# Second layer's channel mixer of a hybrid trunk: two up units on the scaled input, rstd applied to their rows, and the last gate's adaLN steps as rows on VectorE

## Chip, core and metric

One core of one Trainium2 chip runs the whole program. The metric is the device time of one execution in microseconds (us), as the median of three runs. Engines are named as in the profile: PE is TensorE's matmul, PEld its weight load, DVE is VectorE, ACT is ScalarE, POOL is GpSimd, SP is SyncE, whose queue issues the weight loads.

## What is computed

Two layers over 256 tokens of width 1024. Each layer has a token mixer (three branches, left out here) and a channel mixer. Both start from an RMS norm that is modulated (adaLN) by six vectors of 1024 numbers, computed from a condition vector `c`:

```python
c_act = jax.nn.silu(c)
for l in range(DEPTH):
    mod = c_act @ w_mod[l] + b_mod[l]
    sh1, sc1, g1, sh2, sc2, g2 = jnp.split(mod, 6, axis=-1)
    ...
    x = x + g1[:, None, :] * y
    h = modulate(rms_norm(x, ffn_norm_g[l]), sh2, sc2)
    x = x + g2[:, None, :] * channel_mixer(h, w_up[l], ffn_dw_w[l], ffn_dw_b[l], w_down[l])

def channel_mixer(h, w_up, ffn_dw_w, ffn_dw_b, w_down):
    u = causal_depthwise_conv(h @ w_up, ffn_dw_w, ffn_dw_b)   # width 3
    a, b = jnp.split(u, 2, axis=-1)                           # 2816 each
    return (jax.nn.silu(a) * b) @ w_down
```

The norm's factor rstd is one number for each token. So `h @ w_up` is also `rstd * ((gain * x) @ w_up) + sh2 @ w_up`: the product can start before rstd is known, if rstd is applied to its result and the shift's product is added. That identity is what the changed code uses for two units.

## The kernel before

**Layout.** Channels lie on the 128 partitions and tokens along the free dimension. `x` is 8 tiles (k = 0 to 7) of 128 x 256. The channel mixer's inner width of 2816 is cut into 22 units (j = 0 to 21). `up(j)` makes 128 channels of a and 128 of b; `down(j)` adds unit j's product with `w_down` to 8 output tiles in four PSUM tiles.

**Weights.** A weight load (`wload`, SP's queue) brings 512 KB to a `raw` tile. `split` makes its high half on ACT (`whi`, L222) and the rest on DVE (`wlo`, L224). A product takes three matmuls: high x high and low x high as it goes (L300, L301), and all high x low last (L303). One weight load feeds 24 matmuls, called a unit load here: an `up` takes two unit loads (k = 0 to 3, then 4 to 7), a `down` one. `take` hands out loads in a fixed list (`all_units`) and splits two ahead of their use; the `raw`, `whi` and `wlo` tiles rotate through few buffers, so a load or a split waits until a buffer is let go. L294 to L296 are the three matmuls of the last products of an accumulation, done bank after bank.

**Between the token mixer and the channel mixer.** `project` ends in four PSUM tiles. DVE adds them, gated, to `x` (L1251), ACT squares (L530), DVE adds squares in pairs (L540), PE sums over partitions (L545), DVE and POOL make rstd (L519, L520), PE spreads it over the partitions (L555, `bcast_rows`), and then each of 8 `norm_tile` steps takes DVE, ACT, DVE (L603, L604, L605) and gives `hh` and `hl`, the halves of h. While this chain runs, PE has nothing to multiply but `mod_part(l, 5)` (L407: the vector g2, 8 steps, each with its own 512 KB load of `in_wm`) and filler matmuls on a constant (`warm`, L322).

**After an `up`.** ACT scales and biases the PSUM tile (L1298), DVE adds the two shifted taps (L1300, twice for each of a and b), ACT makes the tanh (L1304), DVE multiplies (L1305, L1306), ACT and DVE write the high and low half that `down(j)` reads (L1308, L1309; tile `mhl`). Three PSUM buffers (`psb`) serve the `up` units, so `up(j+3)` waits until the taps of `up(j)` have been read. Five buffers (`psa`) serve the accumulations.

**Order.** The list `FFN` sets how `up` and `down` alternate: up 0, 1, 2, down 0, up 3, 4, down 1, up 5, down 2 and so on, so `up` runs three ahead and later four. A scheduler with a cost model of its own turns the program into one fixed row of instructions for each engine; `tc.issue_after` adds edges to it. On the chip every engine goes through its row in order.

**adaLN as rows.** Where (layer, vector) stands in `ROWS`, the vector is made on DVE: `mod_row` loads 512 KB of transposed weights and does one multiply with a running sum over 1024 elements (L390) and one add (L391), 8 times for a vector. In layer 0's channel mixer 16 such steps for the next layer run beside `up` and `down`.

Of the kernel before, what the change touches and what calls it, by code (L numbers as in the profile page):

```python
# [64 lines left out]
ROWS = [(0, 0), (0, 1), (1, 0), (1, 1), (1, 2)] + RPARTS  # L65
# [68 lines left out]
FFN = []  # L134
for _j in range(NF):
    for _u in range(NF):
        if (1, _u) not in FFN and _u <= _j + (3 if _j >= FLEAD else 2):
# [16 lines left out]
def trunk_kernel(ctx, tc, xT, crow, ccol, pos, invf, modb_d, cols_d, grow_d, wmh, wmr, wm, win1, wqkv,  # L154
# [60 lines left out]
    def split(raw, lead):  # L215
# [7 lines left out]
        with tc.issue_after(hold[0]) if hold[0] else ExitStack():  # L223
            ve.tensor_tensor(lo, raw, hi.bitcast(F32), op=ALU.subtract)  # L224
# [63 lines left out]
    def flush(whole=False):  # L288
        if whole:
# [233 lines left out]
    def sq_sums(srcs, bank=None):  # L523
# [3 lines left out]
        alone = SHORT and n == 8  # L527
        for k, src in enumerate(srcs):
            sq = e1()
            ac.activation(sq, src, AF.Square)  # L530
# [12 lines left out]
            with tc.issue_after(warm(bank, WARM1[0]).ins) if bank is not None and WARM1[0] and k == n - 2 + (not alone) else ExitStack():  # L543
# [8 lines left out]
    def bcast_rows(r):  # L552
        bc = psb()
        for b in range(NB):
            rows_last[0] = te.matmul(bc[:, b * P:(b + 1) * P], r[:, b:b + 1].to_broadcast([P, P]), ident,  # L555
                                     start=True, stop=True)
# [44 lines left out]
    def norm_tile(k, bc, gs, sh, hh, hl):  # L601
        t = e1()
        ve.scalar_tensor_tensor(t, x[:, k, :], gs, bc, op0=ALU.mult, op1=ALU.mult)  # L603
# [1 line left out]
        v = ve.scalar_tensor_tensor(hl[:, k, :], t, sh, hh[:, k, :].bitcast(F32), op0=ALU.add, op1=ALU.subtract)  # L605
# [135 lines left out]
    def layer(l):  # L741
# [508 lines left out]
        for n in range(KD):  # L1250
# [3 lines left out]

        gs2 = mod_gain(l, 4, "ffn_g")
        fill = mod_part(l, 5)
        bc = norm_stats(fill)
        hh, hl = new_h()
        marks = [norm_tile(k, bc, gs2[:, k:k + 1], mod[l][:, 24 + k:25 + k], hh, hl) for k in range(KD)]
        fw = wk.tile([P, 3, 44], F32, tag="fw", name=nm("fw"), bufs=1)  # L1260
        fb = wk.tile([P, 44], F32, tag="fb", name=nm("fb"), bufs=1)
        with tc.issue_after(marks[0][1].ins):
# [21 lines left out]
        lo_tags[:] = [("wlo", 4), ("qkT", 2), ("wlo", 4), ("kv", 2)] if l else [("wlo", 4), ("qkT", 2), ("wlo", 4), ("kv", 2), ("wlo", 4), ("qkT", 2), ("wlo", 4), ("thc", 1)]  # L1284
        def up(j):
            pp = psb()
            for _ in range(2):
                for k, w in take()[0]:
                    for i in range(2):
                        mmw(pp[:, i * S:(i + 1) * S], cut(w, i, P), (hh[:, k, :], hl[:, k, :]), k == 0 and i == 0,  # L1290
                            k == KD - 1 and i == 1)
                flush()
# [132 lines left out]
```

## Time and profile before

| | |
|---|---|
| time, median of 3 runs | 907.75 us (905.73 to 909.3) |
| the profiled execution: time, span | 909.82 us, 907.7 us |
| PE busy, DVE busy, ACT busy over the span | 98%, 88%, 61% |
| projection of layer 1 ends on PE | 711.5 us |
| first matmul of layer 1's `up(0)` | 718.93 us |
| layer 1's `down(1)` starts, `up(5)` starts | 751.93 us, 754.76 us |
| last matmuls of the program | about 904 us |

Times are from the span's start. A row of the timeline reads: start, duration, engine, line, operation, output tile <- input tiles, shape, count, and in brackets the idle time before it with what ended it. The durations of neighbouring rows overlap a little, because each instruction's record reaches into the next one's start; what an instruction costs its engine is read from start to start. A busy PE in the table of stretches is not a PE at its peak either, since its records overlap by more than half.

### The profile page before, as it was taken

The page shows a single profiled execution, that of the slowest core. Times are in us where ns is not written, and L with a number is a line of the kernel's source. Part 1 is how long each engine was busy: PE and PEld are TensorE (multiplying, and loading weights), DVE is VectorE, ACT ScalarE, POOL GpSimd, SP SyncE. Part 2 cuts the span into 40 slices and gives each one's busy share as a digit, 9 for nine tenths or more (in the row PEclk, how much of TensorE's full clock was granted, in tenths as well). Part 3 has the DMA queues.
Part 4 walks back from the last instruction along what each step waited for, and adds up shares of the span by engine and source line. Part 5 has one row for each costly group of instructions (what it writes and reads, how often), then busy time and mean ns, then how long its engine had stood idle before and what let it go on. Part 6 is the DMA issues. An engine that isn't in the chain of part 4 may idle for free.

```text
span 907.7 us, 18736 instructions
## 1 busy us (share of the span) xinstructions
PE 888.3 (98%) x7339; PEld 841.5 (93%) x7339; DVE 797.1 (88%) x1554; ACT 555.2 (61%) x979; POOL 46.2 (5%) x36
## 2 busy tenths in 40 slices
PE   7999999999999999999999999999999999999998
PEld 6888888999998999999989988989999899999998
DVE  6989999999988999998764999999887798777774
ACT  4677588644755655556543676986475565565551
POOL 1010700000000000000000043000000000000000
PEclk9999999999999999999999999999999999999999
DMA  8956535699988889996633664157768676566631
GB/s 321 379 196 202 187 118 183 214 334 320 304 292 308 295 296 312 313 301 211 200 112 108 197 223 161 53 184 244 264 206 270 221 259 189 186 194 199 190 92 47
DMA packets 57976, 201.59 MB, mean 222 GB/s; under 512 B 6944, under 2 KB 8480, under 8 KB 57888
## 3 DMA queue, kind: packets, MB, share of 16 engines
q1 hardware_dynamic: 57888, 200.41, 66.6%
q8 instruction: 57, 0.93, 0.4%
q14 instruction: 31, 0.25, 0.1%
HBM read 199.33 MB, written 1.05 MB: 221 GB/s over the span
## 4 chain that ended last, share of the span: by engine, by line
PE 78%; DVE 12%; ACT 4%; DMA 3%; issue 2%; SPq 0%; POOL 0%; POOLq 0%; DVEq 0%; ACTq 0%
PE psb L300 16%; PE psb L301 16%; PE psb L303 15%; PE psa L300 7%; PE psa L301 7%; PE psa L303 7%; DVE wlo L224 3%; DVE cacc L1103 3%; PE psa L407 2%; DVE raw L778 1%; ACT whi L222 1%; PE psa L294 1%; DVE raw L390 1%; DMA raw<-in_win 1%; ACT p L675 1%
## 5 line engine op out<-in xcount | busy, mean ns | idle before, releaser
L222 ACT ACTIVATE whi<-raw 128x1024 fp32r<-128x1024 f32 (+2 forms) x286 | 296.6, 1043 | 217.6 <-PE psb L301 117.3
L224 DVE TENSOR_TENSOR wlo<-raw,whi 128x1024 fp32r<-128x1024 f32 (+2 forms) x286 | 340.3, 1195 | 65.5 <-ACT whi L222 57.9
L300 PE MATMUL psb<-hh,whi 128*128 128x256 f32 x1088 | 263.5, 282 | 0.5 <-ACT p L675 0.3
L301 PE MATMUL psb<-hl,whi 128*128 128x256 f32 x1088 | 261.0, 280 | 0.0
L300 PEld LDWEIGHTS psb<-hh,whi 128*128 128x128 f32 x1088 | 205.0, 189 | 6.3 <-issue 3.8
L301 PEld LDWEIGHTS psb<-hl,whi 128*128 128x128 f32 x1088 | 205.0, 189 | 0.5 <-DVE wlo L224 0.4
L303 PE MATMUL psb<-hh,wlo 128*128 128x256 f32 x1088 | 149.2, 279 | 0.0
L303 PEld LDWEIGHTS psb<-hh,wlo 128*128 128x128 f32 x1088 | 135.6, 188 | 0.8 <-issue 0.8
L1103 DVE SCALAR_TENSOR_TENSOR cacc<-upad,cw,cacc 128x256 f32<-128x256 f32 x240 | 105.7, 477 | 0.4
L300 PE MATMUL psa<-mhl,whi 128*128 128x256 f32 x400 | 94.0, 278 | 0.0
L301 PE MATMUL psa<-mhl,whi 128*128 128x256 f32 x400 | 93.7, 278 | 0.0
L1300 DVE SCALAR_TENSOR_TENSOR e<-psb,fw,e 128x255 f32<-128x255 f32 (+1 forms) x176 | 84.0, 477 | 5.4 <-ACT e L1298 4.5
L520 POOL TENSOR_TENSOR rs<-rs,mhalf 128x8 f32<-128x8 f32 (+3 forms) x26 | 44.6, 1729 | 669.2 <-DVE rs L519 669.1
L300 PEld LDWEIGHTS psa<-mhl,whi 128*128 128x128 f32 x400 | 75.0, 188 | 0.0
L301 PEld LDWEIGHTS psa<-mhl,whi 128*128 128x128 f32 x400 | 75.0, 188 | 0.0
L1298 ACT ACTIVATE e<-psb,fb,fw 128x256 f32<-128x256 f32 x88 | 48.5, 551 | 22.4 <-DVE e L1300 19.2
L390 DVE SCALAR_TENSOR_TENSOR raw<-raw,crow 128x1024 f32<-128x1024 f32 x48 | 58.5, 1218 | 0.5 <-DMA raw<-in_wmr 0.5
L303 PE MATMUL psa<-mhl,wlo 128*128 128x256 f32 x400 | 53.9, 277 | 0.0
L303 PEld LDWEIGHTS psa<-mhl,wlo 128*128 128x128 f32 x400 | 49.4, 188 | 0.0
L1308 ACT ACTIVATE mhl<-e 128x256 fp32r<-128x256 f32 x44 | 18.3, 416 | 30.1 <-DVE e L1306 27.6
L300 PE MATMUL psb<-whi,hh 128*128 128x416 f32 (+1 forms) x96 | 30.9, 350 | 4.5 <-ACT hh L854 4.5
L301 PE MATMUL psb<-whi,hl 128*128 128x416 f32 (+1 forms) x96 | 29.6, 343 | 0.2 <-DVE hl L855 0.2
(275 smaller groups left out, 1474.3 us busy)
## 6 DMA issues: line engine op xcount, KB each, us to landing
raw<-in_wup SPq DMA_DIRECT2D x88, 512.0 KB, 4.9
raw<-in_wmr SPq DMA_DIRECT2D x60, 512.0 KB, 5.7
raw<-in_wdn SPq DMA_DIRECT2D x44, 512.0 KB, 4.5
raw<-in_wm SPq DMA_DIRECT2D x32, 512.0 KB, 4.7
raw<-in_wgab SPq DMA_DIRECT2D x32, 512.0 KB, 4.9
raw<-in_wqkv SPq DMA_DIRECT2D x24, 512.0 KB, 5.1
raw<-in_win SPq DMA_DIRECT2D x16, 512.0 KB, 4.7
raw<-in_wgc SPq DMA_DIRECT2D x16, 512.0 KB, 4.3
```

The source lines that it names most:

```text
L222: ac.activation(hi, raw, AF.Copy)
L224: ve.tensor_tensor(lo, raw, hi.bitcast(F32), op=ALU.subtract)
L300: te.matmul(o, p1[0], p1[1], start=start, stop=False)
L301: te.matmul(o, p2[0], p2[1], start=False, stop=False)
L303: te.matmul(o, p3[0], p3[1], start=False, stop=stop)
L390: ve.scalar_tensor_tensor(raw, raw, scale, row, op0=ALU.mult, op1=ALU.mult, accum_out=acc)
L407: te.matmul(acc[32 * c:32 * c + 32, 0:S], cact[:, k:k + 1].to_broadcast([P, 32]), raw[:, c * S:(c + 1) * S], start=(k == 0), stop=(k == KD ...
L520: gp.tensor_tensor(r, r, mhalf[:, :n], op=ALU.pow)
L1103: ve.scalar_tensor_tensor(aj, upad[:, j, t:t + S], cw[:, j * 31 + t:j * 31 + t + 1], aj, op0=ALU.mult, op1=ALU.add)
L1298: ac.activation(t, src, AF.Identity, scale=fw[:, 2, c:c + 1], bias=fb[:, c:c + 1])
L1300: ve.scalar_tensor_tensor(t[:, d:S], src[:, 0:S - d], fw[:, 2 - d, c:c + 1], t[:, d:S], op0=ALU.mult, op1=ALU.add)
L1308: ac.activation(mh, th, AF.Copy)
```

## The change

In layer 1 alone, the channel mixer's start is rewritten. `raw_tile` forms u = gain * x (without rstd) in high and low halves as soon as a tile of `x` is complete, 256 columns and two more that hold the shift (`raw_operand`). `up(0)` and `up(1)` (`NRAW = 2`) multiply that u, 258 columns wide, each into two `psa` tiles, half by half: `raw_unit(0)`, `raw_unit(1)`, the sums over partitions, `raw_unit(0)` again, the spreading of rstd, `raw_unit(1)` again. Their results are multiplied by rstd's row on DVE, and the shift's product (column 256) is added on ACT. `norm_tile` still makes `hh` and `hl`, now for `up(2)` onward. The filler matmuls and `mod_part(1, 5)` leave PE; g2 comes from eight `mod_row` steps. `bcast_rows` uses a transpose in place of a matmul with the identity. The order of layer 1 becomes up 0 to 4, down 0, up 5, down 1, up 6: `up` runs four ahead from the start.

```diff
-ROWS = [(0, 0), (0, 1), (1, 0), (1, 1), (1, 2)] + RPARTS
+ROWS = [(0, 0), (0, 1), (1, 0), (1, 1), (1, 2), (1, 5)] + RPARTS
...
-            FFN.append((1, _u))
-    FFN.append((0, _j))
+NRAW = 2
+FFN = [_ffn(2, 3), _ffn(4, 4)]
...
     def split(raw, lead):
-        with tc.issue_after(hold[0]) if hold[0] else ExitStack():
+        after = holds.pop(0) if holds else hold[0]
+        with tc.issue_after(after) if after else ExitStack():
             ve.tensor_tensor(lo, raw, hi.bitcast(F32), op=ALU.subtract)
...
+            if l == 1:
+                for i in range(2):
+                    for j in range(NRAW):
+                        yield *chop(wup[l, j], KD, S)[i], LEAD
...
     def bcast_rows(r):
-            rows_last[0] = te.matmul(bc[:, b * P:(b + 1) * P], r[:, b:b + 1].to_broadcast([P, P]), ident,
-                                     start=True, stop=True)
+            rows_last[0] = te.transpose(bc[:, b * P:(b + 1) * P], r[:, b:b + 1].to_broadcast([P, P]), ident)
...
+    def raw_tile(k, gs, uh, ul):
+        ac.activation(uh[k][:, 0:S], x[:, k, :], AF.Identity, scale=gs[:, k:k + 1])
+        return ve.scalar_tensor_tensor(ul[k][:, 0:S], x[:, k, :], gs[:, k:k + 1], uh[k][:, 0:S].bitcast(F32),
+                                       op0=ALU.mult, op1=ALU.subtract)
...
+        else:
+            taps()
+            uh, ul = raw_operand(mod[l][:, 24:32])
+            st = psb()
+            sums = []
+            for n in range(KD):
+                residual(n)
+                sq = e1()
+                ac.activation(sq, x[:, n, :], AF.Square)
+                if n % 2:
+                    ve.tensor_tensor(sums[-1], sums[-1], sq, op=ALU.add)
+                else:
+                    sums.append(sq)
+                last = raw_tile(n, gs2, uh, ul)
+            pre.extend([psa(), psa()] for _ in range(NRAW))
+
+            def raw_unit(j):
+                for k, w in take()[0]:
+                    for i in range(2):
+                        mmw(pre[j][i][:, 0:S + 2], cut(w, i, P), (uh[k], ul[k]), k == 0, k == KD - 1)
+                return flush()
...
+            holds[:] = [last.ins]
+            mid = raw_unit(0)
+            holds.clear()
+            behind[0] = 1
+            with tc.issue_after(mid.ins):
+                mid = raw_unit(1)
+            for i in range(4):
+                with tc.issue_after(mid.ins):
+                    mid = total(i)
+            r = rstd_of(st[:, 0:NB], NB, 1.0 / D)
+            holds[:] = [rst[0].ins]
+            with tc.issue_after(mid.ins):
+                mid = raw_unit(0)
+            holds.clear()
+            with tc.issue_after(mid.ins):
+                bc = bcast_rows(r)
+            hh, hl = new_h()
+            for k in range(KD):
+                marks.append(norm_tile(k, bc, gs2[:, k:k + 1], mod[l][:, 24 + k:25 + k], hh, hl,
+                                       marks[k - 2] if k > 1 else None))
+            holds[:] = [marks[3][1].ins]
+            with tc.issue_after(rows_last[0].ins):
+                raw_unit(1)
...
-        rows_left = [(1, r, k) for r in range(2) for k in range(KD)] if l == 0 else []
+        rows_left = [(1, r, k) for r in ((5,) if l else range(2)) for k in range(KD)]
...
+                if raw:
+                    src = e1()
+                    ve.tensor_tensor(src, pre[j][i][:, 0:S], bcs, op=ALU.mult)
+                    cb = small(1, "m0", 4)
+                    ve.tensor_copy(cb, pre[j][i][:, S:S + 1])
+                    ac.activation(src, src, AF.Identity, bias=cb)
+                else:
+                    src = pp[:, i * S:(i + 1) * S]
...
-            if j > 1 and rows_left:
+            if j > (8 if l else 1) and rows_left:
                 mod_row(crow1[0], *rows_left.pop(0), scale=0.5 if CDMA else 1.0)
```

The fixed rows of the engines show where this puts the work. In the changed kernel the matmul lines 300, 301, 303 are 317, 318, 320 and `split`'s DVE line 224 is 231; the evacuation's lines 1300, 1305, 1306, 1309 are 1409, 1414, 1415, 1418. The number behind a name only tells tiles apart.

TensorE right behind layer 1's projection, before (`psa_1574_9317` is the sum of `mod_part(1, 5)`, `psb_1578_9331` that of the squares):

```order
L296 MATMUL psa_1502_8812<-mhl_1558_9179,wlo_1562_9188 128x256
L407 MATMUL psa_1574_9317<-raw_1575_9318,cact_106 32x256 x4
L407 MATMUL psa_1574_9317<-raw_1576_9324,cact_106 32x256 x4
L545 MATMUL psb_1578_9331<-ones_84,e1_1579_9332 128x1 x2
L545 MATMUL psb_1578_9331<-ones_84,e1_1581_9339 128x1 x2
```

The same place in the changed kernel (`psa_1590_9371` and `psa_1591_9372` are the a and b halves of `up(0)`, `u_1576_9315` and `u_1578_9317` hold u's high and low half):

```order
L313 MATMUL psa_1502_8812<-mhl_1558_9179,wlo_1562_9188 128x256
L317 MATMUL psa_1590_9371<-u_1576_9315,whi_1564_9193 128x258
L318 MATMUL psa_1590_9371<-u_1578_9317,whi_1564_9193 128x258
L317 MATMUL psa_1591_9372<-u_1576_9315,whi_1564_9193 128x258
L318 MATMUL psa_1591_9372<-u_1578_9317,whi_1564_9193 128x258
```

The products of `up(0)` stand directly behind the projection; the sums of squares come 48 matmuls later.

VectorE around the low half of the second unit's activation, before (`mhl_1628_9605`, read by `down(1)`):

```order
L417 TENSOR_TENSOR mod1_101<-psa_1630_9610,modb_94 128x8
L1306 TENSOR_TENSOR e1_1627_9601<-e1_1627_9601,e1_1626_9597 128x256
L1300 SCALAR_TENSOR_TENSOR e1_1638_9675<-psb_1631_9614,fw_1605_9450,e1_1638_9675 128x255
L1309 TENSOR_TENSOR mhl_1628_9605<-e1_1627_9601,mhl_1628_9605 128x256
L1300 SCALAR_TENSOR_TENSOR e1_1638_9675<-psb_1631_9614,fw_1605_9450,e1_1638_9675 128x254
```

The same place in the changed kernel (`mhl_1632_9588` is read by `down(1)`; `psb_1633_9591` is the PSUM tile of `up(2)`, `wlo_1688_9936` belongs to `down(2)` and `wlo_1692_9967` to `up(7)`):

```order
L231 TENSOR_TENSOR wlo_1688_9936<-raw_1686_9933,whi_1687_9935 128x1024
L1409 SCALAR_TENSOR_TENSOR e1_1630_9580<-e1_1628_9575,fw_1573_9307,e1_1630_9580 128x255
L1414 SCALAR_TENSOR_TENSOR e1_1631_9584<-e1_1631_9584,e1_1627_9571 128x256
L1409 SCALAR_TENSOR_TENSOR e1_1630_9580<-e1_1628_9575,fw_1573_9307,e1_1630_9580 128x254
L1409 SCALAR_TENSOR_TENSOR e1_1642_9656<-psb_1633_9591,fw_1573_9307,e1_1642_9656 128x255
L1415 TENSOR_TENSOR e1_1631_9584<-e1_1631_9584,e1_1630_9580 128x256
L1409 SCALAR_TENSOR_TENSOR e1_1642_9656<-psb_1633_9591,fw_1573_9307,e1_1642_9656 128x254
L231 TENSOR_TENSOR wlo_1692_9967<-raw_1690_9964,whi_1691_9966 128x1024
L1418 TENSOR_TENSOR mhl_1632_9588<-e1_1631_9584,mhl_1632_9588 128x256
L1409 SCALAR_TENSOR_TENSOR e1_1643_9660<-psb_1633_9591,fw_1573_9307,e1_1643_9660 128x255
L1414 SCALAR_TENSOR_TENSOR e1_1644_9664<-e1_1644_9664,e1_1642_9656 128x256
L1409 SCALAR_TENSOR_TENSOR e1_1643_9660<-psb_1633_9591,fw_1573_9307,e1_1643_9660 128x254
```

The second unit's half now stands among the taps of `up(2)` and behind a split for `up(7)`; the last of the rows lets go the PSUM buffer that `up(5)` takes.

TensorE at `down(1)`, before (`psb_1660_9800` is `up(4)`):

```order
L303 MATMUL psb_1660_9800<-hh_1595_9416,wlo_1652_9728 128x256 x8
L300 MATMUL psa_1642_9690<-mhl_1628_9605,whi_1654_9757 128x256
L301 MATMUL psa_1642_9690<-mhl_1628_9605,whi_1654_9757 128x256
L300 MATMUL psa_1642_9690<-mhl_1628_9605,whi_1654_9757 128x256
L301 MATMUL psa_1642_9690<-mhl_1628_9605,whi_1654_9757 128x256
L300 MATMUL psa_1643_9691<-mhl_1628_9605,whi_1654_9757 128x256
L301 MATMUL psa_1643_9691<-mhl_1628_9605,whi_1654_9757 128x256
```

The same place in the changed kernel (`mhl_1624_9563` is the activation of `down(0)`, `psb_1675_9857` is `up(5)`):

```order
L317 MATMUL psa_1668_9823<-mhl_1632_9588,whi_1673_9829 128x256
L317 MATMUL psa_1669_9824<-mhl_1632_9588,whi_1673_9829 128x256
L317 MATMUL psa_1670_9825<-mhl_1632_9588,whi_1673_9829 128x256
L317 MATMUL psa_1671_9826<-mhl_1632_9588,whi_1673_9829 128x256
L318 MATMUL psa_1668_9823<-mhl_1632_9588,whi_1673_9829 128x256
L317 MATMUL psa_1668_9823<-mhl_1632_9588,whi_1673_9829 128x256
L318 MATMUL psa_1668_9823<-mhl_1632_9588,whi_1673_9829 128x256
L318 MATMUL psa_1669_9824<-mhl_1632_9588,whi_1673_9829 128x256
L317 MATMUL psa_1669_9824<-mhl_1632_9588,whi_1673_9829 128x256
L318 MATMUL psa_1669_9824<-mhl_1632_9588,whi_1673_9829 128x256
L317 MATMUL psb_1675_9857<-hh_1603_9475,whi_1659_9750 128x256
```

Ten matmuls of `down(1)`, of which the fifth is the first to read the low half, now stand directly behind `down(0)` and ahead of `up(5)`.

More of the change, by code (lines that the diff above doesn't have):

```diff
@@ L130, with _ffn @@
 NCOL = _o
[L134 to L137, printed above, removed]
-            FFN.append((1, _u))
-    FFN.append((0, _j))
+def _ffn(first, then):
+    o = []
+    for j in range(NF):
+        for u in range(NF):
+            if (1, u) not in o and u <= j + (then if j >= FLEAD else first):
+                o.append((1, u))
+        o.append((0, j))
+    return o
+NRAW = 2
+FFN = [_ffn(2, 3), _ffn(4, 4)]
 def _two_pi_parts():
@@ L207, in trunk_kernel @@
     hold = [None]
+    holds = []
     raw_tags = [("raw", 4)]
@@ L302, in flush @@
         for o, _, _, p3, _, stop in queue:
-            te.matmul(o, p3[0], p3[1], start=False, stop=stop)
+            last = te.matmul(o, p3[0], p3[1], start=False, stop=stop)
         queue.clear()
+        return last
     def cut(w, i, n):
@@ L542, in sq_sums @@
                     continue
-            with tc.issue_after(warm(bank, WARM1[0]).ins) if bank is not None and WARM1[0] and k == n - 2 + (not alone) else ExitStack():
+            with tc.issue_after(warm(bank, WARM1[0]).ins) if bank is not None and WARM1[0] and k == n - 1 else ExitStack():
                 for b in range(NB):
@@ L1249, in layer, with residual, taps @@
         ve.tensor_scalar(g1h, mod[l][:, 16:24], 0.5, None, op0=ALU.mult)
-        for n in range(KD):
+        def residual(n):
             ve.scalar_tensor_tensor(x[:, n, :], acc[n // 2][:, (n % 2) * S:(n % 2 + 1) * S], g1h[:, n:n + 1],
                                     x[:, n, :], op0=ALU.mult, op1=ALU.add)
[L1255 to L1262, printed above, removed]
+        def taps():
             wsrc = cv(l, "fdw_w").rearrange("p (t j) -> p t j", t=3)
@@ L1283, in layer @@
         hi_tags[:] = [("whi", 4), ("mq", 3)]
-        lo_tags[:] = [("wlo", 4), ("qkT", 2), ("wlo", 4), ("kv", 2)] if l else [("wlo", 4), ("qkT", 2), ("wlo", 4), ("kv", 2), ("wlo", 4), ("qkT", 2), ("wlo", 4), ("thc", 1)]
+        lo_tags[:] = [("wlo", 4), ("qkT", 2), ("wlo", 4), ("kv", 2), ("wlo", 4), ("qkT", 2), ("wlo", 4), ("thc", 1)]
         def up(j):
[L1286 to L1292, printed above, removed]
+            raw = j < len(pre)
+            if not raw:
+                pp = psb()
+                for _ in range(2):
+                    for k, w in take()[0]:
+                        for i in range(2):
+                            mmw(pp[:, i * S:(i + 1) * S], cut(w, i, P), (hh[:, k, :], hl[:, k, :]), k == 0 and i == 0,
+                                k == KD - 1 and i == 1)
+                    flush()
             ab = []
```

82 lines of the change are left out of this document (63 added, 19 removed).

## The prediction

> **What bounds the kernel now.** I read the page first, for which engine the end hangs on, then the stretches, to see whether that holds around the change, then the timelines of TensorE and VectorE from layer 1's projection to `down(1)`.
>
> ```profile
> PE 888.3 (98%) x7339; PEld 841.5 (93%) x7339; DVE 797.1 (88%) x1554; ACT 555.2 (61%) x979; POOL 46.2 (5%) x36
> PE 78%; DVE 12%; ACT 4%; DMA 3%; issue 2%; SPq 0%; POOL 0%; POOLq 0%; DVEq 0%; ACTq 0%
> 360.00:380.00 20.00, 20.00 (x179) 20.00 (x178) 20.00 (x40) 10.73 (x17) 0.00 (x0) 1.00 0.94 310
> 720.00:740.00 20.00, 19.88 (x175) 18.55 (x174) 19.41 (x35) 14.34 (x23) 0.00 (x0) 1.00 0.76 253
> 780.00:800.00 20.00, 20.00 (x176) 20.00 (x175) 15.52 (x26) 11.99 (x18) 0.00 (x0) 1.00 0.60 189
> ```
>
> Line 1 and the chain (line 2, 78% PE) say TensorE. But a mean hides the stage: in the rows of stretches (PE, PEld, DVE, ACT, POOL, then PEclk, DMA share and GB/s) VectorE is busy 19.41 of 20 us at 720 to 740, right behind the place of the change, and 15.52 at 780 to 800. So TensorE bounds, with VectorE nearly full for some 25 us. What counts is which of the two the change loads there.
>
> ```profile
> 711.24 0.28 PE L296 MATMUL psa<-mhl,wlo 128*128 128x256 f32 x1
> 711.45 1.07 PE L407 MATMUL psa<-raw,cact 128*32 128x256 f32 x16
> 712.45 1.05 PE L545 MATMUL psb<-ones,e 128*128 128x1 f32 x8
> 713.36 0.60 PE L322 MATMUL psb<-warm_w 128*128 128x256 bf16 x4
> 713.95 1.05 PE L545 MATMUL psb<-ones,e 128*128 128x1 f32 x8
> 714.87 0.93 PE L322 MATMUL psb<-warm_w 128*128 128x256 bf16 x7
> 716.10 0.71 PE L555 MATMUL psb<-ident,rs 128*128 128x128 f32 x4 [0.30 <-POOL rs L520]
> 716.64 0.49 PE L322 MATMUL psb<-warm_w 128*128 128x256 bf16 x3
> 718.93 0.39 PE L300 MATMUL psb<-hh,whi 128*128 128x256 f32 x1
> 751.93 0.28 PE L300 MATMUL psa<-mhl,whi 128*128 128x256 f32 x1
> 754.76 0.28 PE L300 MATMUL psb<-hh,whi 128*128 128x256 f32 x1
> 788.67 0.28 PE L300 MATMUL psb<-hh,whi 128*128 128x256 f32 x1
> 791.39 0.28 PE L300 MATMUL psb<-hh,whi 128*128 128x256 f32 x1
> ```
>
> TensorE's timeline: the projection's last matmul ends at 711.52, `up(0)` starts at 718.93, `down(1)` at 751.93, `up(5)` at 754.76. One unit load lies between the last two: 2.83 us for 24 matmuls, or 0.118 each; between 788.67 and 791.39 it is 2.72. So much for TensorE: 40.41 us from 711.52 to 751.93 hold 11 unit loads (up 0 to 4, `down(0)`), 31.1 us, and 9.3 us of other things.
>
> ```profile
> 707.50 0.87 DVE L1251 SCALAR_TENSOR_TENSOR x<-psa,g1h,x 128x256 f32<-128x256 f32 x2
> 715.04 0.16 DVE L519 TENSOR_SCALAR rs<-psb 128x2 f32<-128x2 f32 x1 [0.81 <-PE psb L545]
> 716.85 1.26 DVE L603 SCALAR_TENSOR_TENSOR e<-x,gs,psb 128x256 f32<-128x256 f32 x3 [1.64 <-PE psb L555]
> 718.03 0.88 DVE L605 SCALAR_TENSOR_TENSOR hl<-e,mod,hh 128x256 fp32r<-128x256 f32 x2
> 724.72 3.48 DVE L224 TENSOR_TENSOR wlo<-raw,whi 128x1024 fp32r<-128x1024 f32 x3
> 728.13 0.47 DVE L1300 SCALAR_TENSOR_TENSOR e<-psb,fw,e 128x255 f32<-128x255 f32 x1
> 728.52 1.21 DVE L224 TENSOR_TENSOR wlo<-raw,whi 128x1024 fp32r<-128x1024 f32 x1
> 731.57 0.41 DVE L1305 SCALAR_TENSOR_TENSOR e<-e,e 128x256 f32<-128x256 f32 x1
> 731.91 0.47 DVE L1300 SCALAR_TENSOR_TENSOR e<-psb,fw,e 128x254 f32<-128x254 f32 x1
> 734.89 1.23 DVE L224 TENSOR_TENSOR wlo<-raw,whi 128x1024 fp32r<-128x1024 f32 x1 [0.59 <-ACT whi L222]
> 741.17 0.42 DVE L1309 TENSOR_TENSOR mhl<-e,mhl 128x256 fp32r<-128x256 f32 x1
> ```
>
> VectorE's timeline, start to start: a split 3.41 / 3 = 1.137, a norm step 1.18 / 3 = 0.393 (716.85 to 718.03), a tap 0.39, a multiply 0.34. From the norm's first step to the half that `down(1)` reads (L1309 at 741.17) it takes 24.3 us with 0.59 idle. TensorE comes to `down(1)` 10.4 us later. That slack is what the change spends.
>
> **The change, part by part.** *TensorE's start.* Out go g2's product (L407), the fillers (L322) and the waits between, and `up(0)` follows the projection. It needs u's low halves, which VectorE now makes between the residual adds: from 707.50, the start of those adds, to the fourth low half stand 7 adds, 4 low halves and 2 sums of squares at 0.39 to 0.43 each, and a split: 5.5 + 1.14 = 6.6, so about 714.2 with little idle, and 714.5 at TensorE. The unit load would have asked for it at 711.52 + 12 x 0.113 = 712.9: 1.5 us of wait, ends near 715.7. `raw_unit(1)` 2.72: 718.4. The sums over partitions, without what stood between: (713.36 - 712.45) + (714.87 - 713.95) = 1.83: 720.3. `raw_unit(0)`'s second half 2.72: 723.0. Spreading 716.64 - 716.10 = 0.54 with the transpose (its price is not in the trace; between 0 and a double 1.1 I take the old one): 723.6. Added up without further waits, `down(1)` could start at 711.5 + 1.5 + 31.1 + 1.8 + 0.5 = 746.5 instead of 751.93: **5.4 us earlier**. The 258th column and its neighbour are 0.8% on 96 matmuls, under 0.1 us.
>
> *VectorE's start.* The norm steps begin when rstd is spread: 723.6 instead of 716.64, **6.9 us later**, because one and a half units now stand ahead of the spreading. Behind L519 in VectorE's row stand only a split and then the norm steps, so it idles meanwhile.
>
> *VectorE from there to the half for `down(1)`.* I count the changed row of instructions: 16 norm steps (6.3), 13 splits (14.8), 4 multiplies by rstd's row at a norm step's 0.39 at most, I take 0.36 (1.4), 4 copies of a column (0.4), 10 taps (3.9), 6 multiplies and low halves (2.0): 28.8, against 24.3 - 0.6 before. With the same 0.6 idle the half is there at 723.7 + 29.4 = 753.1.
>
> *SP's queue.* Two of g2's loads now stand ahead of `down(0)`'s; their tiles are u's, free only when `raw_unit(1)`'s second half is done at 726.3, and `down(0)`'s own buffer is free when a split of `up(4)` ends, near 728.8.
>
> ```profile
> raw<-in_wdn SPq DMA_DIRECT2D x44, 512.0 KB, 4.5
> L222 ACT ACTIVATE whi<-raw 128x1024 fp32r<-128x1024 f32 x19 | 19.9, 1057 | 10.9 <-PE psb L301 7.8 <-DMA raw<-in_wdn 1.2 <-PE psa L301 1.0
> L390 DVE SCALAR_TENSOR_TENSOR raw<-raw,crow 128x1024 f32<-128x1024 f32 x48 | 58.5, 1218 | 0.5 <-DMA raw<-in_wmr 0.5
> ```
>
> The load lands 4.5 us after its issue (its row among the DMA issues), ACT takes 1.06: 734.4. That split stands in VectorE's row ahead of the last low half of h, and is due after 8 norm steps, 7 low halves and 2 splits, near 732.8. All behind it slips by about 1.5 (0 if the load is issued early, 4.5 if it waits a landing more): the half for `down(1)` is there near **754.8**, and its PSUM buffer's last taps (L1409 twice, L1414 once) let go at 756.0.
>
> *What TensorE does with that.* First wait: `up(2)`'s last k reads the last low half of h, at about 735.9, where TensorE is ready for it at 730.6. Then up 3, 4 and `down(0)` to 751.3, four matmuls of `down(1)`, and the second wait, to 754.8. Six more, and `up(5)` starts at 756.0 when its buffer is free, with 14 of `down(1)`'s 24 matmuls still owing (14 x 0.118 = 1.65). Before, `up(5)` started at 754.76 with nothing owing. So the change costs 756.0 + 1.65 - 754.76 = **+2.9 us**: 5.4 us of TensorE's work saved, 8.3 us of waiting put in.
>
> *g2's rows.* Eight steps of 1.218 on VectorE (L390), from `up(9)` on. In layer 0, rows 360 to 380, the same steps run with VectorE at 20.00 of 20 and TensorE also 20.00 of 20; at 780 to 800 4.5 us of 20 are free on VectorE, and a step comes once in 3 unit loads (8.2 us). Cost 0, covered by those 4.5; if that cover were gone, 8 x 1.2 = 9.7 on VectorE. The loads are as many and as large as those of g2's old product. `up` running four ahead instead of three has the end of layer 1 in hand: 0.
>
> Sum: 909.82 + 2.9 = 912.7 against the profiled execution, whose time is 2.07 above the median of the runs shown (907.75). Against that median: 910.6.
>
> **Rivals.** *VectorE keeps pace* (the other side). If the splits ahead of TensorE's use cost VectorE less, or down(0)'s load is early, and the half for `down(1)` is there before TensorE asks, the whole 5.4 shows: 902.4. It decides at the half's time: at 746.5 all is saved, at about 752 nothing is lost or won. For it: before, the same half had 10.4 us to spare. Against: a start 6.9 later, 5.1 of added work and 1.5 of slip are 13.5, and TensorE asks 5.4 sooner.
>
> *Waiting slows the clock.*
>
> ```profile
> 468.00:470.00 2.00, 1.96 (x11) 1.43 (x15) 0.71 (x2) 0.20 (x1) 0.00 (x0) 0.52 0.71 264
> 470.00:472.00 2.00, 2.00 (x28) 0.90 (x27) 2.00 (x6) 1.11 (x3) 0.00 (x0) 0.62 0.00 0
> ```
>
> At the layer boundary, where TensorE also has little to multiply, the granted clock falls to 0.52 and 0.62 over two stretches of 2 us: 2 x 0.48 + 2 x 0.38 = 1.7 us of work lost. Layer 1's start has no such dip now (its fillers are what the change takes away). With waits of 5.3 and 3.5 us one such dip at 735.9 would shorten the second wait and cost little; one at 754.8 costs all of 1.7: 912.3. In the Trainium skill, "TensorE: Matmul & The Clock Gate", section "What's actually happening", the clock is halved after at least one idle window of about 3.4 us and comes back after such a window of work; by that the dip would be an estimated 1.7 us, for each wait that long. The trace agrees that the clock halves, and has no wait of 5 us that would try the length.
>
> *The slower step stays.* TensorE's unit loads come in two steps, 2.83 (751.93 to 754.76) and 2.72 (788.67 to 791.39), and 788.67 stands 12 unit loads behind 754.76. If what is waited for leaves it in the slow step, the 42 of layer 1's 66 unit loads that are left then cost 42 x 0.11 = 4.6 more: 915.2. For it: nothing in the rows says why it changes. Against: TensorE is busy 19.88 of 20 us at 720 to 740, ahead of the slow step at 751.93, so the slow step is no mark of a wait.
>
> *The waits eat just the saving.* If the slip on SP's queue and the late PSUM buffer are each a little shorter, 907 to 908: no change.
>
> **How the numbers follow.** The forecast (910.6, itself 909.1 to 913.6 by the slip's bounds, 1.5 below and 3.0 above) 0.45; VectorE keeps pace 0.15 (902.4); the clock 0.12 (912.3); the slower step 0.15 (915.2); just eaten 0.13 (907.5). The range runs to the outer cases: 902.5 to 915.3. 0.5% or 4.5 us, about what a measurement of this kernel can tell from no change, puts faster below 903.2 and slower above 912.3. Faster 0.16 (the first rival, and 0.01 of the last), slower 0.27 (the slower step, half of the clock's case, and 0.06 from the forecast's upper part), the same 0.57.
>
> **What would show it.** Right: the first matmul of `up(0)` within 0.3 us of 711.5; the norm's first step at 723 to 724; TensorE idle for VectorE's low half of h in `up(2)` near 731 to 736 and for L1418 in `down(1)` near 752 to 755; `up(5)` near 756; behind it the same time per unit load, and the end 2 to 4 us later. Wrong: no idle TensorE at `down(1)`, and all later times 5 us earlier (VectorE was faster than counted, or its instructions wait less); waits at `up(0)` far above 1.5 us (u's halves are late); a granted clock under 0.9 behind the waits; unit loads of 2.83 beyond 790; or VectorE idle for g2's loads in the later units, which would make the eight rows cost something.

## The result and the profile after

| | before | after |
|---|---|---|
| time, median | 907.91 us (11 runs, 905.73 to 911.98) | 912.15 us (11 runs, 910.45 to 917.22) |
| ratio, 95% interval | | 1.0054 (1.0032 to 1.0075) |
| profiled execution, span | 909.82 us, 907.7 us | 911.17 us, 909.1 us |

The change makes the kernel slower by 4.2 us between the medians, 0.54% by the ratio. Its interval shows that the change costs something, and not whether that is more than the half per cent by which the prediction told slower from the same. The prediction said 910.6, with 902.5 to 915.3 as its range.

The page of the changed kernel, its first row and its chain of work, against the first two lines shown of before:

```profile
PE 882.1 (97%) x7247; PEld 838.5 (92%) x7247; DVE 809.0 (89%) x1596; ACT 558.0 (61%) x994; POOL 47.0 (5%) x36
PE 77%; DVE 11%; DMA 5%; ACT 3%; issue 2%; SPq 0%; POOL 0%; DVEq 0%; ACTq 0%; POOLq 0%
```

TensorE is busy 6.2 us less, and the program is longer: TensorE now waits. This page of the profile does not say where. TensorE's timeline from the end of layer 1's projection does (start, duration, line, operation, tiles, shape, count, wait):

```profile
708.88 0.28 PE L313 MATMUL psa<-mhl,wlo 128*128 128x256 f32 x1
708.99 0.28 PE L317 MATMUL psa<-u,whi 128*128 128x258 f32 x1
711.99 0.51 PE L318 MATMUL psa<-u,whi 128*128 128x258 f32 x2 [0.82 <-DVE u L644]
716.23 1.84 PE L1337 MATMUL psb<-ones,e 128*128 128x1 f32 x16
717.93 0.36 PE L317 MATMUL psa<-u,whi 128*128 128x258 f32 x1
720.92 0.38 PE L570 MATMUL psb<-ident,rs 128*128 128x128 f32 x2
721.05 0.37 PE L317 MATMUL psa<-u,whi 128*128 128x258 f32 x1
732.42 0.65 PE L317 MATMUL psb<-hh,whi 128*128 128x256 f32 x2 [1.62 <-ACT hh L617]
752.45 1.22 PE L317 MATMUL psa<-mhl,whi 128*128 128x256 f32 x4 [4.34 <-ACT mhl L1417]
753.86 0.58 PE L318 MATMUL psa<-mhl,whi 128*128 128x256 f32 x1 [0.19 <-DVE mhl L1418]
755.31 0.41 PE L317 MATMUL psb<-hh,whi 128*128 128x256 f32 x1
761.62 0.28 PE L318 MATMUL psa<-mhl,whi 128*128 128x256 f32 x1
```

In this execution the projection ends at 709.16, 2.36 us sooner than in that of before, for reasons ahead of the change (see the last section), so what follows is counted from there. The raw product starts at once, as it should. Rstd is spread at 720.92 and TensorE stands still three times: 0.82 us for u, 1.62 us in `up(2)`, 4.53 us at `down(1)`, for the second unit's activation. `up(5)` starts 46.2 us behind the projection; before it was 43.2 (754.76 - 711.52), with `down(1)` done, of which 14 matmuls are owing now.

VectorE's timeline, the other side of the last wait, and the row of ACT that lets TensorE go:

```profile
721.33 0.87 DVE L616 SCALAR_TENSOR_TENSOR e<-x,gs,psb 128x256 f32<-128x256 f32 x2 [1.93 <-PE psb L570]
732.00 1.22 DVE L231 TENSOR_TENSOR wlo<-raw,whi 128x1024 fp32r<-128x1024 f32 x1 [1.56 <-ACT whi L228]
742.88 0.42 DVE L1414 SCALAR_TENSOR_TENSOR e<-e,e 128x256 f32<-128x256 f32 x1 [1.21 <-ACT e L1413]
753.39 0.42 DVE L1418 TENSOR_TENSOR mhl<-e,mhl 128x256 fp32r<-128x256 f32 x1
751.98 0.42 ACT L1417 ACTIVATE mhl<-e 128x256 fp32r<-128x256 f32 x1 [1.88 <-DVE e L1415]
```

From the first norm step (721.33) to the low half that `down(1)` reads (753.39) VectorE takes 32.1 us; before it took 24.3. TensorE's long wait names ACT, which writes the high half, but ACT had itself waited 1.88 us for VectorE's multiply (L1415) ahead of it. So it is VectorE's chain, not TensorE's work, that sets when `down(1)` goes.

Last, the clock. Stretches of 2 to 6 us (PE, PEld, DVE, ACT, POOL busy, granted clock, DMA share, GB/s):

```profile
730.00:734.00 4.00, 2.38 (x16) 2.09 (x16) 2.44 (x7) 1.82 (x4) 0.00 (x0) 0.90 0.49 146
734.00:740.00 6.00, 6.00 (x43) 6.00 (x43) 6.00 (x10) 4.86 (x7) 0.00 (x0) 0.78 0.86 246
748.00:750.00 2.00, 0.11 (x1) 0.00 (x0) 2.00 (x2) 1.97 (x5) 0.00 (x0) 1.00 0.82 256
750.00:752.00 2.00, 0.00 (x0) 0.00 (x0) 2.00 (x7) 0.12 (x2) 0.00 (x0) 0.57 0.86 236
752.00:754.00 2.00, 1.36 (x5) 1.07 (x5) 2.00 (x4) 1.70 (x4) 0.00 (x0) 0.50 0.94 287
754.00:756.00 2.00, 2.00 (x10) 2.00 (x11) 2.00 (x7) 0.32 (x1) 0.00 (x0) 0.50 0.69 211
756.00:758.00 2.00, 2.00 (x15) 2.00 (x15) 2.00 (x6) 1.40 (x4) 0.00 (x0) 0.72 0.23 88
```

Behind both waits the clock is halved. The lost clock, summed, is 0.10 x 4 + 0.22 x 6 = 1.72 us, so 3.4 us at half speed, and from 750 on 2 x (0.43 + 0.50 + 0.50 + 0.28) = 3.42 us, so 6.8 us at half speed, of which the first two lie in the wait. The 48 matmuls of `up(5)` take 6.31 us (755.31 to 761.62) where 5.44 is the fast price.

### The profile page after: what moved, and what is told of

The parts are those of the page before. It is cut to its first block, busy times and chain, and to the rows that moved or that the text cites. A ratio compares the mean times of both kernels' runs of the same rounds, so it can differ in the third digit from the quotient of the medians.

```text
span 909.1 us, 18615 instructions
## 1 busy us (share of the span) xinstructions
PE 882.1 (97%) x7247; PEld 838.5 (92%) x7247; DVE 809.0 (89%) x1596; ACT 558.0 (61%) x994; POOL 47.0 (5%) x36
## 4 chain that ended last, share of the span: by engine, by line
PE 77%; DVE 11%; DMA 5%; ACT 3%; issue 2%; SPq 0%; POOL 0%; DVEq 0%; ACTq 0%; POOLq 0%
PE psb L317 15%; PE psb L318 15%; PE psb L320 15%; PE psa L318 8%; PE psa L317 8%; PE psa L320 7%; DVE wlo L231 3%; DVE cacc L1142 2%; ACT whi L228 2%; DMA raw<-in_win 2%; PE psa L425 1%; PE psa L735 1%; PE psa L747 1%; DVE raw L817 1%; PE psa L311 1%
## 5 line engine op out<-in xcount | busy, mean ns | idle before, releaser
L317 PE MATMUL psb<-hh,whi 128*128 128x256 f32 x1056 | 256.3, 283 | 2.1 <-ACT hh L617 1.6
L318 PE MATMUL psb<-hl,whi 128*128 128x256 f32 x1056 | 253.9, 281 | 0.0
L317 PEld LDWEIGHTS psb<-hh,whi 128*128 128x128 f32 x1056 | 199.7, 189 | 7.0 <-issue 3.0
L318 PEld LDWEIGHTS psb<-hl,whi 128*128 128x128 f32 x1056 | 199.8, 189 | 0.8 <-DVE wlo L231 0.4
L320 PE MATMUL psb<-hh,wlo 128*128 128x256 f32 x1056 | 145.0, 279 | 0.0
L320 PEld LDWEIGHTS psb<-hh,wlo 128*128 128x128 f32 x1056 | 131.8, 189 | 0.8 <-issue 0.8
L1409 DVE SCALAR_TENSOR_TENSOR e<-psb,fw,e 128x255 f32<-128x255 f32 (+1 forms) x168 | 79.6, 475 | 4.6 <-ACT e L1407 4.0
L408 DVE SCALAR_TENSOR_TENSOR raw<-raw,crow 128x1024 f32<-128x1024 f32 x56 | 68.0, 1215 | 0.8 <-DMA raw<-in_wmr 0.8
L1407 ACT ACTIVATE e<-psb,fb,fw 128x256 f32<-128x256 f32 x84 | 46.4, 553 | 29.2 <-DVE e L1409 27.2
L1417 ACT ACTIVATE mhl<-e 128x256 fp32r<-128x256 f32 x44 | 18.4, 418 | 43.2 <-DVE e L1415 41.3
```

Source lines behind the costliest of these rows:

```text
L317: te.matmul(o, p1[0], p1[1], start=start, stop=False)
L318: te.matmul(o, p2[0], p2[1], start=False, stop=False)
L320: last = te.matmul(o, p3[0], p3[1], start=False, stop=stop)
L408: ve.scalar_tensor_tensor(raw, raw, scale, row, op0=ALU.mult, op1=ALU.mult, accum_out=acc)
L1407: ac.activation(t, src, AF.Identity, scale=fw[:, 2, c:c + 1], bias=fb[:, c:c + 1])
L1409: ve.scalar_tensor_tensor(t[:, d:S], src[:, 0:S - d], fw[:, 2 - d, c:c + 1], t[:, d:S], op0=ALU.mult, op1=ALU.add)
```

## The experiments

Two theories stood at the start. **V**: VectorE's chain from the spread rstd to `down(1)`'s low half sets the stage, microsecond for microsecond. **C**, on top of it: the halved clock behind the waits. Against them: TensorE's new products are dearer than counted (P), g2's loads hold up SP's queue (S), the order of the units (O), the eight row steps (R). Kernels of one group share their runs of before; that median was 909.54 us for the first four, 907.91 for the next four and 909.78 for the last, so times are compared within a group, and ratios across.

**Four splits held.** `lows[1]` is the low half that `down(1)` reads. g2's row loads are moved as in the fourth experiment, and its row steps stand behind `lows[3]`. The part of the edit that holds the splits:

```diff
+                if l and j == 1:
+                    holds[:] = [lows[1]]
...
+                if l and j == 5:
+                    holds[:] = [lows[1]] * 2
+                if l and j == 6:
+                    holds[:] = [lows[1]] * 2
```

> The changed kernel, but four splits that stood in VectorE's row ahead of the low half of down(1)'s activation (for up(6), down(2), up(7)) are held behind it, and g2's row loads come later on SP's queue. Theory V (the chain on VectorE from the spread rstd to that low half sets when down(1) and up(5) go): the half comes 4 x 1.14 = 4.5 us earlier, TensorE's wait at down(1) falls from 4.3 us to under 1.5, the clock is not halved behind it, and the time falls 4 to 6 us below the changed kernel's: 0.998 to 1.001 of before. Rival P (TensorE's new products are dearer than counted) or S (SP's queue): no change, 1.004 to 1.006 of before.

Measured 907.77 us, 0.9973 of before (0.9950 to 0.9995). Moving four splits, with nothing taken away, turns the loss into a small gain. TensorE's waits of 700 to 775 us, in total, times, and longest:

```profile
PE psa L318 <- ACT mhl L1421: 3.9, 2, 2.7
PE psb L318 <- ACT hh L620: 0.9, 1, 0.9
```

The wait at `down(1)` is 2.7 us, not under 1.5, and 3.4 us of half clock remain. The gain is a little larger than V said (0.998 to 1.001), with an interval that reaches into that range. In the group, the time is 3.8 us below the kernel with g2's loads moved alone (911.57).

**Rstd's multiplies three times.**

```diff
-                    ve.tensor_tensor(src, pre[j][i][:, 0:S], bcs, op=ALU.mult)
+                    for _ in range(3):
+                        ve.tensor_tensor(src, pre[j][i][:, 0:S], bcs, op=ALU.mult)
```

> The changed kernel with each of the four multiplies by rstd's row issued three times (the same result written again): 8 x 0.34 = 2.7 us more for VectorE ahead of down(1)'s low half. Theory V: the half, the wait of TensorE and the end all come 2 to 3.5 us later, 1.008 to 1.009 of before. Rival P (TensorE bounds this stage, VectorE has slack): no change, 1.0054.

Measured 915.93 us, 1.0064 (1.0034 to 1.0093), 4.4 us above the row-load kernel of the same group, which is nearest to the changed kernel. The ratio is below what V said; it is taken against runs of before that were 1.6 us above those of the first measurement. The trace shows why it is more than 2.7: one of g2's row steps (1.14 us, start to start) slipped ahead of the low half as well.

```profile
759.84 1.21 DVE L408 SCALAR_TENSOR_TENSOR raw<-raw,crow 128x1024 f32<-128x1024 f32 x1
760.98 0.42 DVE L1419 TENSOR_TENSOR mhl<-e,mhl 128x256 fp32r<-128x256 f32 x1
```

The chain is 36.6 us, 4.6 more than the changed kernel's 32.1: 2.7 from the multiplies, 1.1 from the row step, 0.7 from longer waits for ACT. TensorE has no more work than it had, so P falls as the cause of the loss.

**Fillers in the wait.**

```diff
+                if l and j == 0:
+                    with tc.issue_after(last.ins):
+                        fills.append(warm(psa(), 30).ins)
...
+                with tc.issue_after(fills[0]) if l and j == 1 else ExitStack():
+                    down(j)
...
+                if l and j == 5:
+                    es.enter_context(tc.issue_after(fills[0]))
```

> The changed kernel with 30 filler matmuls on a constant (4.0 us by 0.93 for 7) between down(0) and down(1), where TensorE waits 4.3 us. Theory C (the wait halves the clock afterwards, on top of V): the low half comes no sooner, but the granted clock stays at 1.00 behind the wait, the time falls 1 to 2.5 us to 1.003 to 1.004 of before, and the runs near 916 to 917 are gone. Without C (the wait alone costs): the same as the changed kernel, 1.0054, or up to 0.5 us worse.

Measured 910.15 us, 0.9997 (0.9975 to 1.0020), 1.4 us below the row-load kernel of its group, with intervals that overlap. In the trace the clock stays at 1.00 from 748 to 758, where it was halved; but waits of 1.1 and 0.7 us are left behind the fillers, and another stretch at half clock follows at 758. So C is borne out in kind: where TensorE multiplies through the wait, the clock is not halved there. Its size is not settled by this time, which by the ratio is lower than C said. The spread of the runs did not narrow (the highest is 916.12); the last section shows where part of it comes from.

**g2's loads later on the queue.** `dmas[-1]` is the load that was issued last.

```diff
-        return use_row(wload_row(l, r, k, tag), row, l, r, k, scale)
+        with tc.issue_after(dmas[-1]) if r == 5 else ExitStack():
+            raw = wload_row(l, r, k, tag)
+        return use_row(raw, row, l, r, k, scale)
```

> The changed kernel, with g2's first two row loads no longer ahead of down(0)'s load on SP's queue but some fifteen loads later. Rival S (they hold up that load): VectorE's 1.56 us of idle at 730 us goes, the end comes 1 to 1.5 us earlier, 1.0035 to 1.0045 of before. Theory V with the buffer as what the load waits for (it is let go by a split that ends at 726.5, the load goes out at 726.57): no change, 1.0054, and the idle stays.

Measured 911.57 us, 1.0014 (0.9994 to 1.0034). SP's timeline of the changed kernel, then of this one, then VectorE's idle here:

```profile
722.29 1.77 SPq L204 DMA_DIRECT2D raw<-in_wmr  x2
726.57 0.33 SPq L204 DMA_DIRECT2D raw<-in_wdn  x1
```

```profile
727.88 0.33 SPq L204 DMA_DIRECT2D raw<-in_wdn  x1
```

```profile
732.65 1.23 DVE L232 TENSOR_TENSOR wlo<-raw,whi 128x1024 fp32r<-128x1024 f32 x1 [0.90 <-ACT whi L229]
```

Counted from the start of the raw product, `down(0)`'s load goes out at 17.58 (726.57 - 708.99) in the changed kernel and at 17.54 (727.88 - 710.34) here: the buffer, let go by a split, is what it waits for, and not the queue. ACT's half of that split starts 3.7 us behind the load's issue instead of 4.3, so the load lands sooner (idle 0.90 instead of 1.56). That less else was in flight then is a guess that was not tested. So S is worth at most the 0.7 to 0.9 us by which the chain is shorter here; the ratio, lower than either theory's, is too coarse to add to that.

**The changed kernel again.**

> The changed kernel itself, once more, as the measure for the other three on the same chip: 1.002 to 1.0055 of before by the first measurement (1.0032 to 1.0075) and by the four variants, whose runs of before were 1.6 us slower than the first ones.

Measured 913.70 us, 1.0057 (1.0038 to 1.0077): the first result holds.

**Rstd earlier, six splits held.** The spreading (`hook` holds `bcast_rows`) stands behind 10 matmuls of `raw_unit(0)`'s second half; `down(0)`'s split, its high half on ACT included (`holds_hi`), goes behind the last norm step; the splits for the second half of `up(5)` and for `down(1)` are held too.

```diff
+            if hook and i == 4:
+                with tc.issue_after(mid.ins):
+                    hook.pop()()
...
+                if l and j < 2:
+                    holds[:] = [lows[1]] * 2
...
+                if l and j == 3:
+                    holds[:] = [None, marks[-1][1].ins]
+                    holds_hi[:] = [None, marks[-1][0].ins]
+                if l and j == 4:
+                    holds[:] = [None, lows[1]]
+                if l and j in (5, 6):
+                    holds[:] = [lows[1]] * 2
```

> The changed kernel with g2's row loads late, rstd spread after 10 of the 24 matmuls of raw_unit(0)'s second half in place of all 24, down(0)'s split behind the last norm step, and six splits (for the second half of up(5), down(1), up(6), down(2), up(7)) behind the low half that down(1) reads. Theory V: rstd's row is there 1.5 us sooner, 6.8 us of splits leave the chain, TensorE waits under 2 us at down(1) instead of 4.3 and under 0.5 at up(2), and no 3.4 us stretch falls to half clock: 0.993 to 0.996 of before. Rival A (ACT's high halves and tanh, which waited on loads in between, bound the chain now): no better than the version with four splits held, 0.997.

Measured 905.54 us, 0.9966 (0.9947 to 0.9986): just outside what V said, and next to the 0.997 that rival A said. The waits of TensorE fell as expected (1.8 us at `down(1)`, none at `up(2)`), and no stretch from 704 to 768 us is below full clock. But rstd's row is there only 0.9 us sooner, and the chain is still 26.2 us, 3.9 of it idle, all waiting for ACT. (The 4.9 in the last experiment's expectation counts 1.1 us in which VectorE waits for the spreading, ahead of the chain.) One of these waits:

```profile
744.62 1.00 DVE L1425 SCALAR_TENSOR_TENSOR e<-e,fw,e 128x255 f32<-128x255 f32 x2 [1.02 <-ACT e L1423]
```

**g2 as rows alone, on the kernel before.**

```diff
-ROWS = [(0, 0), (0, 1), (1, 0), (1, 1), (1, 2)] + RPARTS
+ROWS = [(0, 0), (0, 1), (1, 0), (1, 1), (1, 2), (1, 5)] + RPARTS
...
-        fill = mod_part(l, 5)
+        fill = None if l else mod_part(l, 5)
```

> The kernel before with g2's part of the change alone: eight row steps from up(9) on in place of mod_part(1, 5); the layer starts as before, with its fillers. Theory V (the rows are covered, the loss is the start's): TensorE loses two groups of g2's matmuls inside up(0) and some 1 us ahead of rstd, 0.998 to 1.000 of before. Rival R (the rows on VectorE or their loads cost in the later units): 1.002 to 1.005.

Measured 905.94 us, 0.9980 (0.9961 to 0.9999). The row steps cost nothing, as predicted, and taking g2's product off TensorE is worth a little. R falls, and so the loss of the change lies in its start.

**The order of before.**

```diff
-FFN = [_ffn(2, 3), _ffn(4, 4)]
+FFN = [_ffn(2, 3), _ffn(2, 3)]
```

> The changed kernel with the order of layer 1 as before (up 0, 1, 2, down 0, up 3, 4, down 1, up 5). Theory V: the low half for down(0) is there at about 745 at best, TensorE reaches down(0) at about 733, and it waits some 8 to 12 us in all, in part given back by splits that stand later: 1.008 to 1.016 of before. Rival O (the order is what costs, the raw units are fine): 0.997 to 1.001.

Measured 907.73 us, 1.0011 (0.9988 to 1.0035). This expectation failed. It took the list for TensorE's row; in fact the scheduler still puts `down(0)` behind 130 matmuls of `up`, at 742.99. What the list did change is the order of weights and so of splits: 10 stand in the chain in place of 13, and it is 28.2 us long. So rival O was right that the order costs (its range ended at 1.001); the chain shows how, by the splits ahead of the low half, which is V.

**ACT's high halves held as well**, on the version with rstd early.

```diff
-            ac.activation(mh, th, AF.Copy)
+            highs.append(ac.activation(mh, th, AF.Copy).ins)
...
+                    if j:
+                        holds_hi[:] = [highs[1]]
...
+                    holds_hi[:] = [None, highs[1]]
...
+                    holds_hi[:] = [highs[1]] * 2
```

> The version with rstd spread early and six splits held, with ACT's high halves for the second half of up(5), for up(6) and up(7) held as well, behind the high half that down(1) reads. Rival A (VectorE's 4.9 us of idle in that chain are waits for ACT, which makes high halves of weights nobody needs yet): the chain from the first norm step to down(1)'s low half shortens from 26.2 to 23 to 25 us, the 1.8 us wait at down(1) goes, 1 to 2 us faster than that version, 0.9945 to 0.996 of before. Rival B (what is left is bound by TensorE's own work): no change, 0.9966.

Measured 904.02 us, 0.9940 (0.9917 to 0.9964): faster than both kernels, though the interval overlaps that of the version without these holds. VectorE's idle in the chain falls from 3.9 to 1.5 us, so the waits were for ACT, as A said. TensorE's waits from 700 to 800 us are down to two, at the start, and none at `down(1)`:

```profile
PE psa L325 <- DVE u L658: 0.8, 1, 0.8
PE psb L584 <- POOL rs L552: 0.6, 1, 0.6
```

**All in one table.** Chain: from the first norm step to the low half for `down(1)` on VectorE's timeline. Stage: from the end of the projection (first g2, sum or raw matmul) to the last matmul of the program, against before (903.73 - 711.45 = 192.28 us), each from one profile.

| kernel | splits in the chain | chain, us | stage against before, us | ratio |
|---|---|---|---|---|
| before | 10 | 24.3 | 0 | 1 |
| rstd three times | 13, 1 row step | 36.6 | +8.7 | 1.0064 |
| after, twice | 13 | 32.1, 32.3 | +3.9, +3.4 | 1.0054, 1.0057 |
| fillers in the wait | 13 | 32.1 | +4.7 | 0.9997 |
| g2's loads later | 13 | 31.3 | +3.1 | 1.0014 |
| four splits held | 9 | 28.3 | +0.1 | 0.9973 |
| order of before | 10 | 28.2 | -1.1 | 1.0011 |
| rstd early, six held | 7 | 26.2 | -3.5 | 0.9966 |
| ACT's halves held too | 7 | 23.7 | -4.1 | 0.9940 |
| g2 as rows alone | 8 | 23.1 | -4.2 | 0.9980 |

The first and the last row start without raw units: there the first norm step comes 5.3 us behind the projection, in the others 11.3 to 12.2, so their chains do not compare with the rest. Among the rest, from 36.6 to 28.3, a microsecond of chain is a microsecond of stage (8.3 against 8.6). That is V, with C's share in it: by the granted clock, half speed lasts 13.7 us from 745 to 770 in the longest, 3.4 us in the shortest. The fillers' stage falls out of line; its profile is that of the slowest of its runs, with two stretches at half clock. In the kernel with ACT's halves held TensorE no longer waits at `down(1)`, so the chain has no more to give; part of its gain is hidden in this profile by a half-clock stretch around the spreading (0.77, 0.50 and 0.88 from 720 to 726) and by the slower step until 778. The ratios go the same way with a scatter of 0.1 to 0.3% (0.5% for the fillers). The last row asks a question that these runs do not answer: moving g2 alone gives as large a stage gain in its profile, which ran at the faster step throughout, and a third of the gain by the ratio. What the raw units are worth on top of it is the 0.4% between two ratios of different groups.

## Why the prediction was right

It named the place, the mechanism and the sign. Step by step, from the end of the projection:

- *TensorE's start.* The wait for u was 0.82 us for 1.5, the sums 1.70 for 1.83, the spreading 0.13 for 0.54 (it became a transpose). Against that, 24 matmuls of the raw unit took 2.9 to 3.0 us (717.93 to 720.92) and not 2.72: the forecast took the faster step for them, while 24 matmuls of `up(3)` ran at 2.83 (737.86 to 740.69) in the same stage. So the 258 columns, costed at under 0.1 us on 96 matmuls, go with at most 0.1 to 0.2 for each unit load, and the step with the rest. In all the first norm step came 12.2 us behind the projection; the sum had 12.2.
- *VectorE's chain.* The count of 28.8 us was right; the idle was sized too small. 0.6 + 1.5 was allowed and 3.4 came: `down(0)`'s split (1.56, predicted 1.5), a tanh of ACT (1.21, not foreseen) and two waits for hh (0.66). `down(1)`'s half was there 1.3 us later than predicted, counted from the projection. (The prediction's own sum, 753.1 and a slip of 1.5, is 754.6 and not 754.8; that changes nothing here.)
- *SP's queue.* The slip was right, half of its cause was wrong: the two row loads ahead of it did not hold up its issue, and by the kernel without them made its landing 0.6 to 0.7 us later.
- *The waits.* The one at `up(2)` was 1.62, predicted 5.3, and for ACT's high half. What it waited for was on time: the last low half of h was there 24.5 us behind the projection, counted at 24.4. TensorE came later: it stood at that wait 21.6 us behind the projection (730.8) and not 19.1, although the raw units were done at 14.9, counted at 14.8. In TensorE's fixed row 16 matmuls of `up(3)` stand ahead of the product that waits, and 8 of `up(4)` behind it, ahead of the last low half's; the prediction counted `up(2)` alone. That step was wrong, and it cost the forecast nothing, because the wait at `down(1)` took up the difference. The one at `down(1)` was 4.5, predicted 3.5, first 4.34 for the high half and then 0.19 for the low one.
- *The clock.* The forecast took no cost for it, and a rival (0.12) said one dip behind `down(1)` would give 912.3; 912.15 was measured. A granted clock under 0.9 behind the waits was also one of the signs of being wrong, and it came. In this profile the dip came at both places, in the second profile of the changed kernel behind the second wait alone. The first is hidden by the second wait, as the rival's text said. Behind `down(1)` it cost `up(5)` 0.9 us. The 10 matmuls before it took up to 0.21 each, but four of them ran while the low half was still awaited, and `up(5)`'s buffer was let go only at about 754.9 (the tap at 754.46); `up(5)` started at 755.31, so 0.4 us more is the clock's. These 1.3 us are the term of the sum that was left out. That the two times nearly agree is luck: the rival put 1.7 us on the forecast's chain, and the chain was longer.
- *The slower step.* It went the other way: behind the wait nearly all unit loads are at 2.72, while before ran at 2.83 until 785. From the start of `up(6)` to 785 that gave back 0.6 us (22.07 against 22.67 for eight unit loads).
- *g2's rows* at 0: confirmed by the kernel that has them alone.

Sum: the forecast had the changed kernel 2.9 us behind when the same 14 unit loads are done (`up(0)` to `up(5)`, `down(0)`, `down(1)`); 5.2 were measured (763.21 - 709.16 against 760.41 - 711.52), 1.3 of the difference from VectorE's chain, 0.4 and 0.9 from half clock ahead of and in `up(5)`, less 0.3 for the faster step there. Then 0.6 comes back by 785, and 0.7 in the last 96 matmuls, why stays open. That leaves +3.9 in this profile, +3.4 in the second and +4.2 in the medians. So the forecast's +2.9 is as near as it is partly by luck: 2.3 us too little up to `up(6)`, 1.3 of it given back by a step and an end that the sum did not hold.

The rival "VectorE keeps pace" named 746.5 as the point where all would be saved. Counted from the projection that is 35.0 us; the last experiment gets to 35.3 by order alone (745.96, projection at 710.7), and its time is 0.6% below before, which is the 5.4 us that the rival said for that case.

## What to carry to other kernels

Work that is taken off the bounding engine is worth only what the next engine's chain lets through: count that engine's instructions in the stage, start to start, between the event that the change delays and the result that the bounding engine waits for next, and add the waits for the third engine. When an in-order engine holds the critical chain, look in its row for work that nobody needs yet. Here holding back six splits and high halves, with rstd spread 14 matmuls sooner and g2's loads issued later, took the version from 0.5% slower to 0.6% faster.

## What was not expected of the hardware

The half-clock stretches of this stage are all 3.4 or 6.8 us long (the shares above give 3.4 and 6.8), and in one execution they stand on a grid: those of the changed kernel begin at 733.2 and 750.3 (from the shares above), 17.1 us apart, which is 5 x 3.41; those of the version with fillers begin at 737.5 and 758.0 (0.88 from 736 to 738; 1.00 from 756 to 758, then 0.50), 20.5 us or 6 x 3.41 apart. A wait need not fill such a window: 1.62 us were enough at `up(2)`, while 0.87 us at the same place with four splits held left the clock at 1.00. Nor does its length alone decide: in the second profile of the changed kernel a wait of 1.64 us at this place left the clock at 1.00 (728 to 740), while one of 1.47 us with the order of before halved it (0.50 from 734 to 736). The grid may decide here, since a wait can fall into one window or across two; that was not tested. The Trainium skill, "TensorE: Matmul & The Clock Gate", section "What's actually happening", halves the clock after at least one idle window of about 3.4 us; the length agrees with these traces, the need for a whole idle window does not.

Part of the scatter of the runs is made ahead of the change. The slowest execution with fillers (916.12 us) starts its raw product at 713.05, 4 us behind the changed kernel's (708.99); of eleven profiles the stage starts between 707.4 and 713.1. Two stretches of layer 0 at its norm, here first and then of the changed kernel, show where some of it went, in clock and waits (0.83 against 1.00):

```profile
220.00:230.00 10.00, 8.28 (x58) 8.11 (x57) 9.19 (x19) 3.92 (x6) 0.86 (x1) 0.83 0.88 301
280.00:290.00 10.00, 9.73 (x88) 6.53 (x89) 9.00 (x23) 8.05 (x13) 0.21 (x1) 0.83 0.75 246
```

```profile
220.00:230.00 10.00, 9.31 (x80) 9.14 (x79) 10.00 (x23) 5.87 (x10) 0.86 (x1) 1.00 0.94 327
280.00:290.00 10.00, 9.92 (x90) 8.76 (x90) 10.00 (x21) 7.83 (x13) 0.00 (x0) 1.00 0.91 319
```

And the two matmul steps differ between executions of the same instructions. In layer 0's channel mixer, which is the same in both kernels, before ran 172 matmuls in 20 us at full clock and after 179:

```profile
300.00:320.00 20.00, 20.00 (x172) 20.00 (x171) 20.00 (x41) 12.59 (x20) 0.00 (x0) 1.00 0.89 293
```

```profile
300.00:320.00 20.00, 20.00 (x179) 20.00 (x178) 20.00 (x42) 11.85 (x19) 0.00 (x0) 1.00 0.89 299
```

What sets it stays open. In this stage it went from 2.83 to 2.72 behind TensorE's waits in the changed kernel, while the version with ACT's halves held, which does not wait there, stayed at 2.83 until 778; but before changed from 2.72 to 2.83 at 731.7 with no wait at all. It moves the stage of a single profile by an estimated 2 us (some 20 unit loads at 0.11 in that of before), so the small differences in the table above, under 26 us of chain above all, are not to be read more finely than the intervals of the ratios.
